# A two-layer streaming encoder: raw weights loaded ahead, the running streams' attention in four steps a pair, and a softmax that joins its two pieces by a reduction

## The chip, the cores and the metric

The kernel runs on one core of a Trainium2 chip. The metric is the device time of one execution in microseconds (us); the figure of merit is the median of three runs. Engines are named as in the profile: PE is TensorE (PEld its weight loads), DVE is VectorE, ACT is ScalarE, POOL is GpSimd, SP is SyncE, whose queue (SPq) issues all DMA transfers of this kernel in one order.

## The reference, cut to what matters

Two layers (`DEPTH = 2`) of width 1024. Each projects its tokens with `w_in`, feeds three groups of attention heads, gates each group, projects the mix with `w_out` and normalises. One call serves two requests with the same weights: 1024 new frames (`prompt`), and 8 running streams of 16 frames with 512 cached frames each (`sample`, 128 rows).

```
h = x @ w_in                                  # split into c_q, c_kv, k_rope, g_mla, f_q, f_k, ..., g_mem
mk, mv = mem @ w_mem_kv                       # 256 memory rows, 4 heads of 64
o_mla = attend(q, k_mla, v, chunk causal)     # 4 heads of 128 + 64 rotary
o_fox = attend(fq, fk, fv, causal, + cq[t] - ck[s])   # 4 heads of 64, with forget sums
o_mem = softmax(mq @ mk.T * scale) @ mv       # 4 heads of 64 over the memory
mixed = concat(o_mla * silu(g_mla), o_fox * silu(g_fox), o_mem * silu(g_mem))
y = layer_norm(alpha * x + mixed @ w_out) * ln_g + ln_b
```

For the sample the same weights are used, and the keys and values of the cache stand ahead of the new ones. The outputs are both `y` and the new cache rows of both layers.

## The kernel before, in words

**Precision and tiles.** Most projections are computed as three matmuls on a high and a low part (`mm3`, L188: L192 high by high, L193 and L194 the crossed ones). `wsplit` (L182) makes the two parts of a weight from its raw load: ACT casts (L183, tile `wh`), then DVE or POOL subtracts (L186, tile `wl`); `self.wdve` says which (1 is DVE, 0 is POOL, 2 takes turns). `WM0 = 2` sets it for the memory weights of layer 0. `split` (L172) does the same for activations (L176 on ACT, L177 on DVE).

**Slots.** Tiles come from pools with a fixed number of slots, and a load into a slot waits until the last reader of its former tile is done: `w` has 8 slots of 128x1024 (raw weights and their halves, tile inputs of the tail, and `lg`/`lb`, the norm's gain and bias), `pw` 5 (`x`, `memx`, softmax rows `pa`, tail inputs `xr`), `ptw` 2 (the transposed probabilities of the prompt's attention), `x` 12 of 128x512 (memory, and the sample's `kT` and `vraw`). The program is written as generators, one piece of background work at each `yield`; a scheduler then sets the order on each engine.

**Start of layer 0.** `main` calls `xload(0)` (L1442: two halves of the first 256 token columns, `x`), then `layer`, whose `gates` (L342) prepares `w_ge` by `wprep` (L259: load raw, split, for two halves of 4x256 rows each) and multiplies it with the tokens, 24 matmuls of 128x256 for each output tile, while `more` loads the other tokens. After `GE0 = 4` steps `mem_prep` (L281) loads `memx` and `w_mk`, projects the memory's keys, then loads `w_mv` and projects its values. Both weights' raw loads go into `w` slots at the place where they are split.

**Middle.** Memory attention, two halves of the forget attention (`fox`), the low-rank projections, then the MLA attention: 16 units (4 heads by 4 pairs of 128 queries, `mla_attn`, L875 on), each a softmax over 128 to 1024 keys in one or two pieces (`soft`, L394). For two pieces DVE takes the maximum of each (L402), joins the two by a 128x1 `tensor_tensor` (L404), ACT exponentiates (L406), DVE joins the two sums (L408), takes the reciprocal (L383), and POOL scales the row in place (L384), which is what PE transposes next (L201); PE then multiplies by the values into the one `pso` slot that DVE reads (L911). At head 3 `wout` (L1211) loads and splits the output weights, `wol` on POOL (L186).

**The sample.** Its attention is a generator, `sample`, that is advanced between other units: kinds `mem`, `fox` and `mla`, for each four pairs of streams. A pair takes one step for each key load, then one for the scores, one for the transposes and the value loads (`s_pv`, L977), one for the value matmuls, one for the output; its scores start when the former pair is finished. The counts `PER`, `PERF`, `PERL`, `PERQ`, `PERT` say how many steps are made at each MLA unit (4), fox unit (1), low-rank step (2), MLA projection (2) and tail tile (8).

**Tail.** Nine tiles of 128 rows: 48 matmuls of 128x512, residual and norm (L1257 to L1265, `lg` and `lb`), and the store of the row, in layer 0 to `yd`. `prep` loads a tile's mix `g` and residual `xr` one tile ahead. In layer 0 the rows of the first four tiles stay in `pw` until they are transposed for layer 1 (`xpair`), the others come back from `yd`. At tiles 4, 6 and 8 (`EM`) the next layer's `mem_prep` is advanced by a step: memory loads and splits, then keys, then values. Then layer 1 starts with `w_ge`.

Of the kernel before, what the change touches and what calls it, by code (L numbers as in the profile page):

```python
# [15 lines left out]
P = 128  # L16
# [4 lines left out]
TS = 16  # L21
# [24 lines left out]
PER = 4  # L46
PERF = 1
BGF = True
PERL = 2
PERQ = 2  # L50
# [19 lines left out]
WM0 = 2  # L70
# [10 lines left out]
class Enc:  # L81
# [40 lines left out]
    def ptw(self):  # L122
        return self.sp.tile([P, 2, 512], F32R, tag="ptw", bufs=T_SLOTS, name=self.nm("ptw"))
# [157 lines left out]
    def mem_prep(self, l):  # L281
        nc = self.nc
        M = []
        for a in range(2):
            raw = self.pw([P, 4, 256], name="memx")
            self.load(raw, self.i["mem_t"][a])
            for b in range(2):
                hi, lo = self.x([P, 2, 256], F32R, "mxh"), self.x([P, 2, 256], F32R, "mxl")
                self.split(hi, lo, raw[:, 2 * b:2 * b + 2, :])
                M.append((hi, lo))  # L290
        yield
# [8 lines left out]
        W = self.wprep(self.i["w_mk"][l])  # L300
# [14 lines left out]
        W = self.wprep(self.i["w_mv"][l])  # L315
# [26 lines left out]
    def gates(self, l, X, src, chunks, more=None):  # L342

        nc = self.nc
        W = self.wprep(self.i[src][l])
# [48 lines left out]
    def soft(self, pss, p, n, col=None, cut=None):  # L394
# [3 lines left out]
        nmx, sm = col(2), col(2)  # L398
        cut = cut or self.cuts(n)
        two = len(cut) == 2  # L400
        for x, (a, b) in enumerate(cut):
            nc.vector.tensor_reduce(nmx[:, x:x + 1], pss[x][:, :b - a], axis=AX, op=ALU.max, negate=True)  # L402
        if two:
            nc.vector.tensor_tensor(nmx[:, 0:1], nmx[:, 0:1], nmx[:, 1:2], op=ALU.min)  # L404
        for x, (a, b) in enumerate(cut):
            nc.scalar.activation(p[:, a:b], pss[x][:, :b - a], AF.Exp, bias=nmx[:, 0:1], accum_out=sm[:, x:x + 1])  # L406
        if two:
            nc.vector.tensor_tensor(sm[:, 0:1], sm[:, 0:1], sm[:, 1:2], op=ALU.add)  # L408
        self.norm(p[:, :n], sm[:, 0:1], col)
# [567 lines left out]
    def s_pv(self, p, nk, src, new, heads):  # L977
# [4 lines left out]
        ph = self.spr()  # L982
        for g in range(0, nkb, 4):
            pt = self.psx()
            k = min(4, nkb - g)
            for a in range(k):
                self.tr(pt[:, a * P:(a + 1) * P], p[:, (g + a) * P:(g + a + 1) * P])
            self.nc.vector.tensor_copy(ph[:, g * P:(g + k) * P], pt[:, :k * P])
        V = [[self.s_256(src(b, a), "vraw") for a in range(nk)] for b in range(2)]
        yield  # L990
        po = self.psx()[:, 0:P if heads else 256]
        for kb in range(nkb):
            first, last = kb == 0, kb == nkb - 1
            for b in range(2):
                v = V[b][kb // 2][:, kb % 2, :] if kb < 2 * nk else new
                if heads:
                    for c in range(2):
                        r = self.s_row(b, c)
                        self.mm(po[r, :], ph[:, kb * P + r.start:kb * P + r.stop], v[:, c * P:(c + 1) * P], first, last)
                else:  # L1000
                    r = slice(b * 64, b * 64 + 64)
                    self.mm(po[r, :], ph[:, kb * P + b * 64:kb * P + b * 64 + 64], v, first, last)
        yield
        s = self.xst([P, 256], name="so")
        w = P if heads else 256
# [26 lines left out]
    def s_mem(self, l):  # L1032
# [577 lines left out]
```

## Time and profile before

| what | value |
|---|---|
| median of 3 runs | 1501.42 us (1500.66 to 1505.01) |
| the profiled execution, its own time | 1506.76 us |
| its span in the profile | 1504.8 us |
| PE busy | 1421.8 us, 94% |
| DVE busy | 777.0 us, 52% |
| ACT busy | 617.8 us, 41% |
| POOL busy | 511.0 us, 34% |
| DMA, mean over the span | 120 GB/s |

The profiled execution is one run, 5.3 us above the median, and 2.0 us of it lie outside the span. A share of busy time is an average: PE leaves only 83.0 us of the span idle, so what is to be read is where these lie and what ended each. A row of a list gives start, duration, engine, line, operation, written tile and read tiles, and in brackets the idle time of the engine just before and what ended it. "PEclk" is the clock granted to PE as a share of full speed in a stretch.

### The profile page before, as it was taken

To read this page: it belongs to the slowest core of one execution; us is meant where nothing else is said; L and a number is where in the kernel's file an instruction comes from. 1 tells how busy PE (TensorE), PEld (TensorE's weight loads), DVE (VectorE), ACT (ScalarE), POOL (GpSimd) and SP (SyncE) were. 2 spreads that over 40 slices of the span, in tenths; PEclk is the share of its full clock that TensorE was granted. 3 is DMA by queue.
4 is the path that set the end of the run, shared out by engine and by line. 5 is a ranking of instruction groups with operands and counts; after the bars stand their busy time and mean duration, and the time that the engine had idled before them with its cause. 6 is when DMAs were issued, how large, how long until landed. Compare 5 with 4: busy or idle time off the path is not lost.

```text
span 1504.8 us, 27868 instructions
## 1 busy us (share of the span) xinstructions
PE 1421.8 (94%) x10222; PEld 1269.3 (84%) x10222; DVE 777.0 (52%) x1957; ACT 617.8 (41%) x1622; POOL 511.0 (34%) x740
## 2 busy tenths in 40 slices
PE   5899999999999999799799999999999999997997
PEld 4899889988987778688689989899889887786886
DVE  4235545255344655757444364552643556567565
ACT  5354445354254444532124453553542544455100
POOL 0233245255262321611141332544433542226012
PEclk9999999999999999999999999999999999999999
DMA  6312342335354431444343223324452643324531
GB/s 246 115 58 72 90 133 65 125 123 152 87 157 156 142 116 34 165 168 144 123 154 98 66 78 112 100 76 120 126 171 65 193 148 119 118 86 143 172 133 56
DMA packets 142343, 180.63 MB, mean 120 GB/s; under 512 B 32384, under 2 KB 99776, under 8 KB 142208
## 3 DMA queue, kind: packets, MB, share of 16 engines
q1 hardware_dynamic: 142208, 178.86, 37.3%
q8 instruction: 81, 1.33, 0.4%
q14 instruction: 54, 0.44, 0.1%
HBM read 138.69 MB, written 40.12 MB: 119 GB/s over the span
## 4 chain that ended last, share of the span: by engine, by line
PE 79%; DMA 8%; DVE 5%; ACT 3%; issue 2%; POOL 2%; SPq 0%; POOLq 0%; DVEq 0%; ACTq 0%
PE pss L192 14%; PE pss L193 13%; PE pss L194 13%; PE pss L197 9%; PE pso L197 7%; PE pst L201 6%; PE psx L197 6%; PE psx L192 3%; PE psx L193 3%; PE psx L194 3%; POOL wl L186 1%; DMA raw<-in_w_kv_dram 1%; ACT wh L183 1%; DMA raw<-in_w_out_dram 1%; PE psx L201 1%
## 5 line engine op out<-in xcount | busy, mean ns | idle before, releaser
L186 POOL TENSOR_TENSOR wl<-raw,wh 128x1024 fp32r<-128x1024 f32 (+3 forms) x42 | 106.5, 2536 | 273.7 <-PE pss L194 77.3
L177 DVE TENSOR_TENSOR ptw<-pst,ptw 128x512 fp32r<-128x512 f32 (+1 forms) x192 | 121.7, 640 | 62.2 <-ACT ptw L176 60.9
L176 ACT CAST ptw<-pst 128x512 fp32r<-128x512 f32 (+1 forms) x192 | 103.2, 550 | 87.4 <-PE pst L201 74.1
L192 PE MATMUL psx<-xh,wh 128*128 128x256 f32 x384 | 110.1, 287 | 16.9 <-ACT wh L183 14.5
L192 PE MATMUL pss<-wh,xh 128*128 128x306 f32 (+1 forms) x384 | 118.4, 308 | 0.0
L193 PE MATMUL pss<-wl,xh 128*128 128x306 f32 (+1 forms) x384 | 117.9, 307 | 0.0
L194 PE MATMUL pss<-wh,xl 128*128 128x306 f32 (+1 forms) x384 | 117.0, 305 | 0.0
L192 PE MATMUL pss<-woh,msh 128*128 128x512 f32 x288 | 115.5, 401 | 1.6 <-DVE xr L1257 1.6
L194 PE MATMUL pss<-woh,msl 128*128 128x512 f32 x288 | 114.7, 400 | 0.0
L193 PE MATMUL pss<-wol,msh 128*128 128x512 f32 x288 | 114.6, 398 | 0.0
L192 PE MATMUL pss<-xh,wh 128*128 128x256 f32 x384 | 111.8, 291 | 0.1
L193 PE MATMUL pss<-xl,wh 128*128 128x256 f32 x384 | 109.5, 285 | 0.0
L194 PE MATMUL pss<-xh,wl 128*128 128x256 f32 x384 | 109.2, 284 | 0.0
L193 PE MATMUL psx<-xl,wh 128*128 128x256 f32 x384 | 109.1, 284 | 0.0
L194 PE MATMUL psx<-xh,wl 128*128 128x256 f32 x384 | 108.5, 285 | 0.1
L384 POOL TENSOR_SCALAR pa<-pa,col 128x128 f32<-128x128 f32 (+3 forms) x64 | 47.8, 750 | 155.0 <-DVE col L383 123.6
L183 ACT CAST wh<-raw 128x1024 fp32r<-128x1024 f32 (+3 forms) x50 | 54.6, 1091 | 109.2 <-DMA raw<-in_w_mk_dram 31.6
L192 PEld LDWEIGHTS psx<-xh,wh 128*128 128x128 f32 x384 | 73.7, 192 | 18.0 <-ACT wh L183 14.7
L197 PE MATMUL pso<-ptw,vh 128*128 128x256 f32 (+1 forms) x336 | 75.0, 297 | 11.4 <-DVE g L911 4.3
L192 PEld LDWEIGHTS pss<-xh,wh 128*128 128x128 f32 x384 | 73.6, 192 | 3.3 <-issue 0.8
L406 ACT ACTIVATE pa<-pss,col 128x512 f32<-128x512 f32 (+3 forms) x96 | 55.3, 581 | 51.2 <-DVE col L404 27.3
L192 PEld LDWEIGHTS pss<-wh,xh 128*128 128x128 f32 x384 | 72.5, 189 | 1.8 <-issue 1.6
(365 smaller groups left out, 4256.1 us busy)
## 6 DMA issues: line engine op xcount, KB each, us to landing
gd<-gg SPq DMA_DIRECT2D x64, 128.0 KB
kT<-in_fox_kt_dram SPq DMA_DIRECT2D x32, 256.0 KB
vraw<-in_fox_v_dram SPq DMA_DIRECT2D x32, 256.0 KB
kT<-in_mla_kt_dram SPq DMA_DIRECT2D x32, 256.0 KB
vraw<-in_mla_v_dram SPq DMA_DIRECT2D x32, 256.0 KB
raw<-in_w_out_dram SPq DMA_DIRECT2D x16, 512.0 KB
g<-md SPq DMA_DIRECT2D x16, 512.0 KB
raw<-in_w_lr_dram SPq DMA_DIRECT2D x8, 612.0 KB
```

The lines of the kernel that those rows point to most:

```text
L176: nc.scalar.copy(hi, ps)
L177: nc.vector.tensor_tensor(lo, ps, self.f(hi), op=ALU.subtract)
L183: self.nc.scalar.copy(hi, raw)
L186: (self.nc.vector if dve else self.nc.gpsimd).tensor_tensor(lo, raw, self.f(hi), op=ALU.subtract)
L192: self.nc.tensor.matmul(ps, ah, bh, start=first and x == 0, stop=False)
L193: self.nc.tensor.matmul(ps, ah, bl, start=False, stop=False)
L194: self.nc.tensor.matmul(ps, al, bh, start=False, stop=last and x == n - 1)
L197: self.nc.tensor.matmul(ps, lhsT, rhs, start=start, stop=stop)
L201: self.nc.tensor.transpose(out, in_, self.ident[:k, :k])
L384: self.nc.gpsimd.tensor_scalar(p, p, rs, 1.0, op0=ALU.mult, op1=ALU.mult)
L406: nc.scalar.activation(p[:, a:b], pss[x][:, :b - a], AF.Exp, bias=nmx[:, 0:1], accum_out=sm[:, x:x + 1])
```

## The change

- **Start.** `xload(0)` issues the raw load of each half of `w_ge` right behind the same half of `x` (`wload`), and `wprep` takes these tiles and splits each in two pieces of 128x512.
- **Memory weights.** `mem_prep` loads the two raw halves of `w_mk` into the two `ptw` slots before its first `yield`, and those of `w_mv` into the same slots as soon as `w_mk` is split. `WM0` is 1: DVE makes the low parts in layer 0.
- **Tail.** `lg` and `lb` lie in `pw` slots, not in `w` slots, so that three of five `pw` slots are left for the tail's rows, `memx` and `x`.
- **Softmax.** The two maxima and the two sums are joined by a 128x2 `tensor_reduce` into a third column, where a `tensor_tensor` of two columns stood.
- **Sample.** `s_pairs` takes four steps a pair: scores, then transposes, then value matmuls, then output. The values of a pair and the keys of the next are loaded in the step of its scores. The counts are `PER` 1, `PERL` 1, `PERQ` 0.

The matmuls are the same in both programs.

The core of the diff (the forms of `s_mem`, `s_fox`, `s_mla` follow `s_pairs`):

```diff
-PER = 4
+PER = 1
 PERF = 1
-PERL = 2
-PERQ = 2
+PERL = 1
+PERQ = 0
-WM0 = 2
+WM0 = 1
-    def ptw(self):
-        return self.sp.tile([P, 2, 512], F32R, tag="ptw", bufs=T_SLOTS, name=self.nm("ptw"))
+    def ptw(self, shape=(P, 2, 512), dt=F32R, name="ptw"):
+        return self.sp.tile(list(shape), dt, tag="ptw", bufs=T_SLOTS, name=self.nm(name))
+    def wload(self, src, alloc=None):
+        parts, _, kn, n = src.shape
+        raws = []
+        for a in range(parts):
+            raw = (alloc or self.w)([P, kn, n if n <= P or n > 256 else 256], name="raw")
+            self.load(raw[:, :, :n], src[a])
+            raws.append(raw[:, :, :n])
+        return raws
-    def wprep(self, src):
+    def wprep(self, src, raws=None, pieces=1):
+        for raw in raws or self.wload(src):
...
-            self.wsplit(hi[:, :, :n], lo[:, :, :n], raw[:, :, :n])
+            for a in range(0, kn, kn // pieces):
+                k = slice(a, a + kn // pieces)
+                self.wsplit(hi[:, k, :n], lo[:, k, :n], raw[:, k])
# mem_prep
+        alloc = lambda shape, name: self.ptw(shape, F32, name)
+        raws = self.wload(self.i["w_mk"][l], alloc)
         yield
...
-        W = self.wprep(self.i["w_mk"][l])
+        W = self.wprep(None, raws)
+        raws = self.wload(self.i["w_mv"][l], alloc)
...
-        W = self.wprep(self.i["w_mv"][l])
+        W = self.wprep(None, raws)
# soft
-        nmx, sm = col(2), col(2)
+        nmx, sm = col(3), col(3)
+        one = slice(2, 3) if two else slice(0, 1)
...
-            nc.vector.tensor_tensor(nmx[:, 0:1], nmx[:, 0:1], nmx[:, 1:2], op=ALU.min)
+            nc.vector.tensor_reduce(nmx[:, one], nmx[:, 0:2], axis=AX, op=ALU.min)
...
-            nc.vector.tensor_tensor(sm[:, 0:1], sm[:, 0:1], sm[:, 1:2], op=ALU.add)
-        self.norm(p[:, :n], sm[:, 0:1], col)
+            nc.vector.tensor_reduce(sm[:, one], sm[:, 0:2], axis=AX, op=ALU.add)
+        self.norm(p[:, :n], sm[:, one], col)
# the sample: s_pairs in place of s_pv and of the steps in s_mem, s_fox, s_mla
+    def s_pairs(self, load, scores, nk, src, new, heads, out):
+        K = load(0)
+        yield
+        for p in range(4):
+            pr = scores(p, K)
+            V = [[self.s_256(src(2 * p + b, a), "vraw") for a in range(nk)] for b in range(2)]
+            if p < 3:
+                K = load(p + 1)
+            yield
...
# tail_start
-        lg = self.w([P, D], name="lg")
+        lg = self.pw([P, D], name="lg")
-        lb = self.w([P, D], name="lb")
+        lb = self.pw([P, D], name="lb")
# xload
+                if j == 0:
+                    raws.extend(self.wload(i["w_ge"][0][kh:kh + 1]))
```

Three places of the order show what moves. The first is SP's queue at the start of layer 0 before; `raw` with `in_w_ge` are the two halves of the gate weights, `x` the token halves, `memx` the memory.

```order
L164 DMA x_102<-in_x_t_dram 128x1024
L164 DMA x_110<-in_x_t_dram 128x1024
L164 DMA raw_139<-in_w_ge_dram 128x1024
L164 DMA x_151<-in_x_t_dram 128x1024
L164 DMA x_159<-in_x_t_dram 128x1024
L164 DMA x_227<-in_x_t_dram 128x1024
```

The next rows of the same queue after some constants, still before:

```order
L164 DMA x_235<-in_x_t_dram 128x1024
L164 DMA qg_5149<-in_mla_q_norm_dram 128x3x1
L164 DMA memx_306<-in_mem_t_dram 128x1024
L164 DMA raw_145<-in_w_ge_dram 128x1024
L164 DMA memx_316<-in_mem_t_dram 128x1024
```

And now, from the first load on:

```order
L164 DMA x_102<-in_x_t_dram 128x1024
L164 DMA raw_104<-in_w_ge_dram 128x1024
L164 DMA x_112<-in_x_t_dram 128x1024
L164 DMA raw_114<-in_w_ge_dram 128x1024
L164 DMA x_155<-in_x_t_dram 128x1024
L164 DMA x_163<-in_x_t_dram 128x1024
L164 DMA x_231<-in_x_t_dram 128x1024
```

The first half of `w_ge` moved from third to second place among the large loads, the second half from behind a `memx` to fourth place. The two `w_mk` loads stand behind the sixth `x` now, ahead of both `memx`.

The second place is SP's queue at the end of layer 0's tail, around tiles 4 to 6; `yd_97` is the store of tile 4's row. Before:

```order
L167 DMA yd_97<-xr_8669 128x1024
L164 DMA xr_9107<-in_x_sample_dram 128x1024
L164 DMA x_9327<-yd_97 128x1024
L164 DMA raw_8948<-in_w_mk_dram 128x1024
L167 DMA yd_98<-xr_8774 128x1024
L164 DMA x_9329<-yd_98 128x1024
L164 DMA raw_8954<-in_w_mk_dram 128x1024
```

And now (the `w_mk` loads, `raw_8800` and `raw_8802`, stand ahead of the store of tile 0):

```order
L164 DMA raw_8964<-in_w_mv_dram 128x1024
L164 DMA xr_8778<-in_x_prompt_dram 128x1024
L164 DMA memx_8780<-in_mem_t_dram 128x1024
L167 DMA yd_97<-xr_8673 128x1024
L164 DMA memx_8790<-in_mem_t_dram 128x1024
L164 DMA xr_8875<-in_x_prompt_dram 128x1024
L164 DMA g_9107<-gtd_142 128x1024
L164 DMA raw_8966<-in_w_mv_dram 128x1024
L164 DMA xr_8948<-in_x_prompt_dram 128x1024
L167 DMA yd_98<-xr_8778 128x1024
```

The `w_mk` loads are no longer behind the read of `yd_97`; the second half of the memory (`memx_8790`) is behind its store, since it takes the slot of the row that `yd_97` stores. On PE the key projection of the next layer begins behind tile 5 in both programs. Before (`pss_8899` is tile 5, `pss_9037` tile 6, `mxh_8778` the high part of the first quarter of the memory, `wh_8950` that of the first half of `w_mk`):

```order
L193 MATMUL pss_8899<-wol_8018,msh_8769 128x512
L194 MATMUL pss_8899<-woh_8017,msl_8770 128x512
L192 MATMUL pss_8960<-wh_8950,mxh_8778 128x256
L192 MATMUL pss_8997<-wh_8950,mxh_8778 128x256
L192 MATMUL pss_9037<-woh_7975,msh_8862 128x512
L193 MATMUL pss_9037<-wol_7976,msh_8862 128x512
```

And now, at the point where it turns to the second memory half (`mxh_8792` is the high part of the first piece of `memx_8790`; `pss_9045` is tile 6):

```order
L192 MATMUL pss_9045<-woh_7924,msh_8870 128x512
L193 MATMUL pss_9045<-wol_7925,msh_8870 128x512
L192 MATMUL pss_8968<-wh_8960,mxh_8792 128x256
L192 MATMUL pss_9005<-wh_8960,mxh_8792 128x256
L193 MATMUL pss_8968<-wl_8961,mxh_8792 128x256
L193 MATMUL pss_9005<-wl_8961,mxh_8792 128x256
L194 MATMUL pss_9045<-woh_7924,msl_8871 128x512
```

Before, two matmuls with the first half of `w_mk` stood right behind tile 5, and ahead of all of tile 6. Now 24 matmuls with the first memory half stand there, then 20 of tile 6, and behind these the first ones with the second memory half.

The third place is POOL in head 3 of the MLA attention of layer 0, where the `wol` subtractions stand between the norms of the probability rows `pa`. Before:

```order
L384 TENSOR_SCALAR pa_7822<-pa_7822,col_7827 128x384
L186 TENSOR_TENSOR wol_7976<-raw_7973,woh_7975 128x1024
L384 TENSOR_SCALAR pa_7837<-pa_7837,col_7842 128x512
L186 TENSOR_TENSOR wol_7982<-raw_7979,woh_7981 128x1024
L384 TENSOR_SCALAR pa_7904<-pa_7904,col_7913 128x896
L186 TENSOR_TENSOR wol_7988<-raw_7985,woh_7987 128x1024
L186 TENSOR_TENSOR wol_7994<-raw_7991,woh_7993 128x1024
L186 TENSOR_TENSOR wol_8000<-raw_7997,woh_7999 128x1024
L384 TENSOR_SCALAR pa_7929<-pa_7929,col_7938 128x1024
```

And now:

```order
L186 TENSOR_TENSOR wol_7889<-raw_7886,woh_7888 128x1024
L186 TENSOR_TENSOR wol_7895<-raw_7892,woh_7894 128x1024
L397 TENSOR_SCALAR pa_7712<-pa_7712,col_7717 128x384
L186 TENSOR_TENSOR wol_7901<-raw_7898,woh_7900 128x1024
L397 TENSOR_SCALAR pa_7727<-pa_7727,col_7732 128x512
L186 TENSOR_TENSOR wol_7907<-raw_7904,woh_7906 128x1024
L397 TENSOR_SCALAR pa_7804<-pa_7804,col_7813 128x896
L186 TENSOR_TENSOR wol_7913<-raw_7910,woh_7912 128x1024
L186 TENSOR_TENSOR wol_7919<-raw_7916,woh_7918 128x1024
L186 TENSOR_TENSOR wol_7925<-raw_7922,woh_7924 128x1024
L397 TENSOR_SCALAR pa_7829<-pa_7829,col_7838 128x1024
```

Two of them are ahead of the 384-key norm (L397 is the former L384), and still three in a row are ahead of the 1024-key norm.

More of the change, by code (lines that the diff above doesn't have):

```diff
@@ new lines, in s_pairs @@
+        w = P if heads else 256
+        K = load(0)
[6 more added lines that the diff above has]
+            yield
+            ph = self.spr()
+            for g in range(0, nkb, 4):
+                pt = self.psx()
+                k = min(4, nkb - g)
+                for a in range(k):
+                    self.tr(pt[:, a * P:(a + 1) * P], pr[:, (g + a) * P:(g + a + 1) * P])
+                self.nc.vector.tensor_copy(ph[:, g * P:(g + k) * P], pt[:, :k * P])
+            yield
+            po = self.psx()[:, 0:w]
+            for kb in range(nkb):
+                first, last = kb == 0, kb == nkb - 1
+                for b in range(2):
+                    v = V[b][kb // 2][:, kb % 2, :] if kb < 2 * nk else new
+                    if heads:
+                        for c in range(2):
+                            r = self.s_row(b, c)
+                            self.mm(po[r, :], ph[:, kb * P + r.start:kb * P + r.stop], v[:, c * P:(c + 1) * P], first, last)
+                    else:
+                        r = slice(b * 64, b * 64 + 64)
+                        self.mm(po[r, :], ph[:, kb * P + b * 64:kb * P + b * 64 + 64], v, first, last)
+            s = self.xst([P, 256], name="so")
+            self.nc.scalar.copy(s[:, 0:w], po)
+            yield
+            pt = self.psx()
+            for c in range(w // P):
+                self.tr(pt[:, c * P:(c + 1) * P], s[:, c * P:(c + 1) * P])
+            out(p, pt)
+            yield
@@ new lines, in load @@
+        def load(p):
+            K = [[self.s_256(kv("fox_kt", 2 * p + b, a), "kT") for a in range(2)] for b in range(2)]
+            ck = self.x([P, 512], name="sck")
+            cn = self.xst([P, TS], name="scn")
+            src = self.cumd[8 * p:8 * p + 8, :]
+            row = lambda a, b: bass.AP(tensor=src.tensor, offset=src.offset + a, ap=[[528, 8], [0, TS], [1, b - a]])
+            self.load(ck, row(0, 512))
+            self.load(cn, row(512, 528))
+            return K, self.s_q(1, 2, p), ck, cn, self.mask(1, p)
@@ L1132, in s_mla @@
+        return self.s_pairs(load, scores, 2, lambda b, a: kv("fox_v", b, a), new[:, 1, :], True,
+                            lambda p, pt: self.s_diag(pt, self.otf, p))
     def s_mla(self, l):
@@ L1179, in sample @@
     def sample(self, l):
[L1181 to L1206 removed]
+        yield from self.s_mem(l)
+        while self.stage < 1:
+            yield
+        self.nc.gpsimd.tensor_copy(self.otf[:, 2:4], self.sx[:, 0, :].rearrange("p (c t) -> p c t", c=2))
+        yield from self.s_fox(l)
+        while self.stage < 2:
+            yield
+        yield from self.s_mla(l)
         self.s_mla_out(l)
@@ L1278, in tail, with layer @@
             outtile(i, *ready[i])
-    def layer(self, l, X, xin, after, early, more=None):
+    def layer(self, l, X, xin, after, early, more=None, raws=None):
         nc = self.nc
@@ L1312, in layer @@
         self.wdve = WG1 if l else 1
-        ge = self.gates(l, X, "w_ge", (6, 7), more)
+        ge = self.gates(l, X, "w_ge", (6, 7), more, raws)
         if l == 0:
```

177 lines of the change are left out of this document (47 added, 130 removed).

## The prediction

> **What bounds the kernel now.** I read the page's busy shares first, then what PE waited for over the whole span, then the stretches in which those waits lie, and in these the rows in order of time.
>
> ```profile
> PE 1421.8 (94%) x10222; PEld 1269.3 (84%) x10222; DVE 777.0 (52%) x1957; ACT 617.8 (41%) x1622; POOL 511.0 (34%) x740
> ```
>
> PE is the bound, and the change leaves its matmuls as they are. So all that can be won is in 1504.8 - 1421.8 = 83.0 us of idle PE, and in the time that a lowered clock stretches its work. The list of what PE waited for (total, times, longest):
>
> ```profile
> PE psx L192 <- ACT wh L183: 17.4, 4, 9.3
> PE pss L192 <- ACT wh L183: 7.8, 2, 6.9
> PE pss L197 <- ACT pa L406: 5.1, 4, 2.3
> PE pso L197 <- DVE g L911: 4.3, 2, 2.2
> PE psx L193 <- POOL wl L186: 4.0, 2, 2.3
> PE pss L192 <- ACT qn L831: 4.0, 2, 3.0
> PE psx L197 <- DMA vraw<-in_mem_v_dram: 1.9, 2, 1.0
> ```
>
> Weights that are not ready (`wh`, `wl`) make 29 us of the 83, and DVE's and ACT's part in the MLA softmax 9. Five stretches hold these waits; a row gives the stretch, its length, PE busy, then the other engines, the granted clock, the DMA share and GB/s:
>
> ```profile
> 0.00:60.00 60.00, 37.83 (x251) 35.22 (x252) 23.55 (x37) 26.96 (x44) 7.50 (x12) 0.89 0.56 193
> 600.00:650.00 50.00, 40.75 (x254) 35.90 (x253) 36.55 (x80) 29.54 (x66) 28.95 (x21) 0.97 0.46 161
> 720.00:740.00 20.00, 12.99 (x50) 9.90 (x48) 7.92 (x13) 1.85 (x3) 1.70 (x2) 0.83 0.52 184
> 740.00:760.00 20.00, 18.55 (x91) 15.31 (x92) 7.49 (x11) 1.05 (x1) 6.28 (x4) 1.00 0.31 105
> 760.00:780.00 20.00, 18.29 (x99) 15.63 (x98) 10.47 (x14) 5.31 (x9) 9.01 (x6) 0.91 0.46 139
> 1350.00:1400.00 50.00, 40.97 (x257) 35.95 (x256) 35.29 (x71) 28.48 (x61) 27.48 (x19) 0.97 0.48 162
> ```
>
> PE idles 22.2 us in the first stretch (60 - 37.83), 10.2 in 720 to 780 (the turn from layer 0 to layer 1), 9.3 and 9.0 in the two stretches of MLA head 3: 50.7 of 83. The change works on all of them.
>
> **The start.** In order of time:
>
> ```profile
> 4.80 2.40 ACT L176 CAST xh<-x 128x512 fp32r<-128x512 f32 x4 [2.80 <-DMA x<-in_x_t_dram]
> 8.23 1.04 ACT L183 CAST wh<-raw 128x1024 fp32r<-128x1024 f32 x1 [1.03 <-DMA raw<-in_w_ge_dram]
> 9.33 0.58 PE L192 MATMUL psx<-xh,wh 128*128 128x256 f32 x1 [9.33 <-ACT wh L183]
> 18.24 1.05 ACT L183 CAST wh<-raw 128x1024 fp32r<-128x1024 f32 x1 [0.16 <-DMA raw<-in_w_ge_dram]
> 19.34 0.58 PE L192 MATMUL psx<-xh,wh 128*128 128x256 f32 x1 [5.22 <-ACT wh L183]
> 37.74 0.39 PE L193 MATMUL psx<-wl,mxh 128*128 128x256 f32 x1 [2.29 <-POOL wl L186]
> ```
>
> The first large load is in at 4.8, the third (half of `w_ge`) at 8.2, so each takes 1.7. As the second load it is in at 6.5; its first piece is cast in half of 1.04, so PE starts at about 7.1 and 2.2 us are gone. The second half is the fourth load, in at 9.9 where it was 18.2, and split by about 12, when PE still has matmuls of the first half (it ran from 9.33 to 14.1 on them, 4.8 us): the gap of 5.22 goes but for some 0.5. The waits for the memory weights, 22.2 - 9.3 - 5.2 = 7.7 with small ones, go where the raw loads are early and DVE takes POOL's place. What is late next: all data come through a queue that is full in this stretch,
>
> ```profile
> 9.33:20.00 10.67, 5.41 (x27) 4.92 (x28) 8.09 (x12) 7.22 (x12) 0.00 (x0) 0.81 0.99 372
> 46.50:53.50 7.00, 5.18 (x23) 4.89 (x24) 0.29 (x1) 1.44 (x3) 3.31 (x3) 0.52 0.21 82
> ```
>
> (DMA share 0.99), and `w_mk` now stands ahead of both `memx`. With six `x`, two `w_ge`, two `w_mk` and two `memx`, the twelfth large load is in at about 4.8 + 11 x 1.7 = 23.5, and `w_mv` behind that. I leave 3.5 us for such new waits. Idle then is 7.1 + 0.5 + 3.5 = 11 against 22.2: 11 gained. The clock: 0.89 over 60 us is 6.6 us of withheld pulses, of which PE's busy share (0.63) is 4.2; I take 3. Sum 14; bounds 8 (new waits of 6.5 and the clock as now, 11 - 3) and 19 (no new wait, whole clock).
>
> The dip at 46.5 to 53.5 came at a clock of 0.52 although PE was busy 5.18 of 7. The Trainium skill, "TensorE: Matmul & The Clock Gate", section "What's actually happening", lets the clock fall only after an idle window of about 3.4 us; PE's longest gap there was under 2, so the trace does not bear the rule out. By the rule no dip would stay at the start and the 4.2 would be gained whole, sum 15; I go by the row, that short gaps close together can do it, and keep a part.
>
> **The turn to layer 1.**
>
> ```profile
> 720.80 0.42 SPq L167 DMA_DIRECT2D yd<-xr  x1
> 725.87 0.33 SPq L164 DMA_DIRECT2D x<-yd  x1
> 726.29 0.38 SPq L164 DMA_DIRECT2D raw<-in_w_mk_dram  x1
> 730.71 1.04 ACT L183 CAST wh<-raw 128x1024 fp32r<-128x1024 f32 x1 [9.60 <-DMA raw<-in_w_mk_dram]
> 730.86 0.33 SPq L167 DMA_DIRECT2D yd<-xr  x1
> 731.81 0.79 PE L192 MATMUL pss<-wh,mxh 128*128 128x256 f32 x2 [6.91 <-ACT wh L183]
> ```
>
> SP's queue waits for the store of tile 4 to land (720.80 to 725.87, 5.07 us) before it may read it back, and `w_mk` is behind that; it lands at 730.7, and PE, two of whose matmuls stand ahead of tile 6, idles from 724.9 to 731.8. Now `w_mk` is loaded before tile 0's store. What is late next is the second memory half: it takes the slot of tile 4's row, so it is issued at about 726, lands at 730.4 (4.4 as above) and is split by about 732 (0.6 on ACT, 0.7 on DVE). Ahead of it PE has 24 matmuls of 128x256 and 20 of 128x512.
>
> ```profile
> L192 PE MATMUL pss<-woh,msh 128*128 128x512 f32 x23 | 9.3, 404 | 1.6 <-DVE xr L1257 1.6
> L192 PE MATMUL pss<-wh,mxh 128*128 128x256 f32 x8 | 2.3, 282 | 0.0
> ```
>
> These are from 740 to 760, with two more rows each for L193 and L194: 67 wide and 24 narrow in 18.55 us, so 18.55 / (67 + 12) = 0.235 a wide one, 0.117 a narrow one. The cover is 24 x 0.117 + 20 x 0.235 = 7.5 us, from 724.9 to 732.4, which just hides it; were tile 6 not there, 7 us would be idle as now. The other rows of tail 0 are read back from `yd` in three slots, and PE's order has their transposes between the first `w_ge` matmuls: up to 4 us may show there. Gain: 10.2 idle plus clock (0.83 in 20 us at a busy share of 0.65, and 0.91 at 0.91: 2.2 + 1.6) is 14.0; I take 9, bounds 4 and 14.
>
> **MLA head 3.** The costs of the join, over both layers, and one chain of time:
>
> ```profile
> L383 DVE RECIPROCAL col<-col 128x1 f32<-128x1 f32 x128 | 20.5, 161 | 37.8 <-ACT pf L420 25.8 <-ACT pa L406 5.9 <-ACT sx L1030 1.4
> L404 DVE TENSOR_TENSOR col<-col 128x1 f32<-128x1 f32 x32 | 16.9, 527 | 0.7
> L408 DVE TENSOR_TENSOR col<-col 128x1 f32<-128x1 f32 x32 | 11.8, 370 | 10.9 <-ACT pa L406 10.7
> 615.99 7.03 POOL L186 TENSOR_TENSOR wol<-raw,woh 128x1024 fp32r<-128x1024 f32 x3
> 616.15 2.20 DVE L404 TENSOR_TENSOR col<-col 128x1 f32<-128x1 f32 x1
> 618.27 0.41 DVE L911 TENSOR_TENSOR g<-pso,g 128x256 f32<-128x256 f32 x1
> 618.83 0.48 PE L197 MATMUL pso<-ptw,vh 128*128 128x256 f32 x2 [2.16 <-DVE g L911]
> 620.80 0.27 DVE L383 RECIPROCAL col<-col 128x1 f32<-128x1 f32 x2
> 624.93 1.87 DVE L404 TENSOR_TENSOR col<-col 128x1 f32<-128x1 f32 x1
> 627.57 0.39 PE L197 MATMUL pss<-xnh,xnh 128*128 128x256 f32 x1 [2.23 <-ACT pa L406]
> ```
>
> An operation on 128x1 needs 0.16, yet L404 needs 2.20 while POOL subtracts `wol`; the reciprocal, with one input in SBUF, runs unhindered in the same POOL burst (620.80). So 16.9 + 11.8 - 64 x 0.16 = 18.5 us of DVE time is being held. The new reduction is not in this trace: between 0.16 (the reciprocal) and 2.20 (L404, held). I take 0.16, since the reciprocal too reads one tile from SBUF. The Trainium skill, "SBUF — State Buffer", section "Who interferes with whom", says that a DVE operation with two SBUF inputs contends with a POOL operation that reads SBUF, and that a `tensor_reduce` on trn2 never does; the trace agrees for the two forms it has, and by the rule the term stays as it is. On the path: the wait of 2.16 falls to some 0.2 (L911 2.0 earlier), that of 2.23 by 1.7 (ACT's `pa` stood behind the join of 1.87), and about 1.3 of the smaller ones: 5 a layer. What stays is POOL's norm behind three `wol` in a row, 7.03 us. Sum 10; bounds 3 (the next waits move up) and 17 (all of 18.3).
>
> **The rest.** Value loads a step earlier remove 1.9 (`vraw`). Sample matmuls leave the low-rank and query steps, where PE waits 4.0 for `qn`, and spread over the MLA units: up to 4 either way, taken at -1. Sum +1.
>
> **The sum.** 14 + 9 + 10 + 1 = 34. The profiled execution took 1506.8, so 1472.8 like for like; it lies 5.3 above the median, so 1467.5.
>
> **The rivals.**
> - *The full queue hides the early weights* (chance 0.15). For it: a DMA share of 0.99 until 20 us. Against: the gap of 5.22 came of the order of the loads, not of their rate, and 22.2 - 9.3 - 5.2 = 7.7 of the idle lies behind that gap. Start 5 in place of 14: 1476.5.
> - *POOL's norm becomes the bound in head 3* (0.15): the 7.03 us of `wol` delay the next probability row whatever DVE does. Against it: PE takes that row a unit later. 0 to 3 in place of 10: about 1476.
> - *Both* (0.07): 1485.
> - *More goes than I allow* (0.05): upper bounds at all three places, 1451.5.
> - *The edits do not reach PE* (0.03): the waits come back elsewhere, within 4 us of 1501.4.
> - *The tail's three slots decide* (0.05), the case on the other side. A slot's round is load 4.4, the tile's matmuls 48 x 0.235 = 11.3, norm 6 (tile 5's matmuls end at 724.9, its store is issued at 730.86), landing 5.07: 26.8, under 3 x 11.3 = 33.9 for three slots. A row that is held 11.3 more for its partner's transposes (tiles 0 to 3 of layer 0) makes 38.1. From 33.9 on PE loses the excess once in three tiles, six times in the two tails; at 41.4, 3.3 more for loads that queue behind a store's landing, that is 6 x 7.5 = 45 lost against 34 won: 1512. Against it: only four of 18 tiles are held.
>
> **The numbers.** The forecast has 0.50, so 1467.5 is the predicted time. The range takes in the two single rivals, their pair and the bounds of the terms that can fall together: 1453 to 1490. Under 0.3% (4.5 us) a measurement of this kernel can't be told from no change: faster 0.92, same 0.03, slower 0.05.
>
> **What would show it.** Right: the first matmul at 7 to 7.5 and no gap over 2 us until 25; no wait for `wh` of 6.9 at the turn; the join at 0.16 to 0.2 while POOL subtracts `wol`, and PE idle of 3 to 5 in each head 3. Wrong: PE waits for `mxh` or `xr` of over 3 us in the tails, a join still over 0.5, or PE idle above 62 us in all.

## The result: 37 us faster, and the profile after

| what | before | after |
|---|---|---|
| median of 4 runs | 1503.22 us (1500.66 to 1505.25) | 1465.78 us (1463.54 to 1469.0) |
| the profiled execution | 1506.76 us | 1465.12 us |
| its span | 1504.8 us | 1463.3 us |
| PE idle in the span | 83.0 us | 54.4 us |

The kernel before has a fourth run here, 1505.25, beside the three shown above. The ratio is 0.9753, 95% interval 0.9727 to 0.978. The predicted time was 1467.5.

First the busy shares on the page of the changed kernel:

```profile
PE 1408.9 (96%) x10222; PEld 1262.3 (86%) x10222; DVE 765.9 (52%) x1961; ACT 617.5 (42%) x1624; POOL 505.6 (35%) x738
```

PE's matmuls are the same 10222, and they take 12.9 us less (1421.8 - 1408.9); idle time fell by 28.6. The two make 41.5, the difference of the spans. The same matmuls take less because the clock is lowered less often (0.984 of full speed over the span before, 0.992 after).

To see where that lies, both programs are cut at places that PE reaches with the same work done: the first matmul of the memory attention, the first score matmul of the MLA attention, its last value matmul, and the same in layer 1. What remains is the tail of layer 1. Of the kernel before (start and end, length, then busy time and count for PE, PEld, DVE, ACT and POOL, then the granted clock, the DMA share and GB/s):

```profile
0.00:74.20 74.20, 52.03 (x371) 49.42 (x372) 25.65 (x42) 30.27 (x51) 11.21 (x14) 0.91 0.54 182
74.20:508.00 433.80, 420.15 (x3345) 388.81 (x3344) 207.43 (x602) 199.11 (x566) 176.42 (x292) 0.99 0.37 111
508.00:665.10 157.10, 147.85 (x978) 122.76 (x977) 96.76 (x249) 74.30 (x190) 48.38 (x47) 0.99 0.38 126
665.10:821.20 156.10, 145.93 (x829) 126.22 (x829) 84.87 (x129) 34.73 (x57) 32.99 (x30) 0.97 0.40 132
821.20:1249.90 428.70, 418.17 (x3347) 386.89 (x3345) 206.88 (x602) 198.91 (x565) 176.28 (x292) 1.00 0.37 113
1249.90:1406.80 156.90, 147.87 (x978) 122.81 (x976) 96.81 (x249) 74.07 (x190) 48.42 (x47) 0.99 0.38 126
```

And the same stretches of the changed kernel:

```profile
0.00:60.60 60.60, 49.95 (x371) 48.66 (x371) 28.15 (x46) 29.87 (x53) 6.81 (x12) 0.94 0.63 223
60.60:490.50 429.90, 415.92 (x3347) 386.23 (x3345) 208.59 (x602) 199.82 (x566) 175.59 (x292) 1.00 0.38 113
490.50:643.20 152.70, 148.72 (x977) 123.30 (x976) 89.00 (x250) 73.44 (x190) 48.30 (x47) 0.99 0.38 125
643.20:785.50 142.30, 141.81 (x830) 123.60 (x830) 85.62 (x128) 34.78 (x57) 33.43 (x30) 1.00 0.45 149
785.50:1213.80 428.30, 415.29 (x3347) 386.33 (x3345) 208.20 (x602) 199.79 (x565) 175.94 (x292) 1.00 0.37 113
1213.80:1365.10 151.30, 147.14 (x977) 121.78 (x976) 88.81 (x251) 73.44 (x190) 48.41 (x47) 1.00 0.40 127
```

PE's counts agree row for row within two, so the lengths may be compared. I call the rows start, middle 0, MLA 0, turn, middle 1 and MLA 1. The start is 13.6 us shorter, the turn 13.8, the two MLA rows 4.4 and 5.6, the middles 3.9 and 0.4. The tail of layer 1 is what is left of each span, 98.0 (1504.8 - 1406.8) and 98.2 (1463.3 - 1365.1). In the turn PE now idles 0.5 us of 142.3, where it idled 10.2, and the clock is whole.

What PE waits for longest in the changed kernel (total, times, longest):

```profile
PE psx L192 <- ACT wh L183: 7.2, 2, 6.6
PE pss L197 <- DVE qf L352: 6.0, 2, 3.3
...
PE pss L197 <- ACT pa L420: 1.7, 4, 0.5
```

The waits for `wh` of 17.4 and 7.8, for `wl` of 4.0, for the join's `pa` of 5.1 and for `qn` of 4.0 are gone or small. What stands at the head is the first load (6.6 of the 7.2), and a wait for `qf`, which I had not looked at; experiment 12 comes back to it.

The start of the changed kernel: ACT's cast of the second half of `w_ge`, and the two matmuls ahead of which PE waited longest.

```profile
9.78 1.14 ACT L183 CAST wh<-raw 128x512 fp32r<-128x512 f32 x2
```

```profile
6.60 0.58 PE L192 MATMUL psx<-xh,wh 128*128 128x256 f32 x1 [6.60 <-ACT wh L183]
...
15.99 0.39 PE L192 MATMUL psx<-xh,wh 128*128 128x256 f32 x1 [1.77 <-DVE gg L376]
```

PE starts at 6.60 where it started at 9.33. The second half of `w_ge` is cast by 10.9, when PE still has matmuls of the first, so the gap of 5.22 is gone. The longest gap left, 1.77, is ended by DVE's gate and not by a weight.

The turn, from the rows of SP's queue and of PE around tile 5:

```profile
696.13 0.37 SPq L164 DMA_DIRECT2D memx<-in_mem_t_dram  x1
697.76 0.33 SPq L167 DMA_DIRECT2D yd<-xr  x1
702.86 0.38 PE L192 MATMUL pss<-wh,mxh 128*128 128x256 f32 x1
703.37 0.33 SPq L164 DMA_DIRECT2D memx<-in_mem_t_dram  x1
```

The second memory half still waits for the store's landing (697.76 to 703.37, 5.61 us), as the prediction had it. But PE begins the keys at 702.86 without a wait for weights, and has the first memory half and tile 6 to work on until the second half is split; no gap over 0.5 is left in the turn.

### The profile page after: what moved, and what is told of

Same layout as the page of the kernel before. It is cut to its first block, busy times and chain, and to the rows that moved or that the text cites. A ratio compares the mean times of both kernels' runs of the same rounds, so it can differ in the third digit from the quotient of the medians.

```text
span 1463.3 us, 27842 instructions
## 1 busy us (share of the span) xinstructions
PE 1408.9 (96%) x10222; PEld 1262.3 (86%) x10222; DVE 765.9 (52%) x1961; ACT 617.5 (42%) x1624; POOL 505.6 (35%) x738
## 4 chain that ended last, share of the span: by engine, by line
PE 80%; DMA 6%; DVE 5%; ACT 3%; POOL 2%; issue 2%; SPq 1%; POOLq 0%; DVEq 0%; ACTq 0%
PE pss L192 13%; PE pss L194 13%; PE pss L193 13%; PE pss L197 9%; PE pso L197 7%; PE pst L201 6%; PE psx L197 6%; PE psx L192 4%; PE psx L194 4%; PE psx L193 4%; SPq L164 1%; PE psx L201 1%; DMA scq<-cumd 1%; DMA raw<-in_w_out_dram 1%; DMA x<-in_x_t_dram 1%
## 5 line engine op out<-in xcount | busy, mean ns | idle before, releaser
L186 POOL TENSOR_TENSOR wl<-raw,wh 128x1024 fp32r<-128x1024 f32 (+3 forms) x40 | 101.5, 2541 | 232.5 <-ACT wh L183 124.1
L397 POOL TENSOR_SCALAR pa<-pa,col 128x128 f32<-128x128 f32 (+3 forms) x64 | 47.9, 757 | 139.5 <-DVE col L396 94.4
L193 PEld LDWEIGHTS pss<-xl,wh 128*128 128x128 f32 x384 | 73.8, 192 | 0.3
```

The source lines that it names most:

```text
L186: (self.nc.vector if dve else self.nc.gpsimd).tensor_tensor(lo, raw, self.f(hi), op=ALU.subtract)
L193: self.nc.tensor.matmul(ps, ah, bl, start=False, stop=False)
L397: self.nc.gpsimd.tensor_scalar(p, p, rs, 1.0, op0=ALU.mult, op1=ALU.mult)
```

## The experiments

All times are medians. "Ratio" is the ratio to the kernel before on the same chip, with its 95% interval. Experiments 1 to 4 ran on one chip, 5 to 8 on another, 9 to 11 on a third, 12 on a fourth. A difference of two ratios from different groups is uncertain by about 0.0035, or 5 us.

### 1. The reduction alone, in the kernel before

The edit is made in the kernel before, in both places of `soft`, and nothing else:

```diff
-            nc.vector.tensor_tensor(nmx[:, 0:1], nmx[:, 0:1], nmx[:, 1:2], op=ALU.min)
+            nc.vector.tensor_reduce(nmx[:, one], nmx[:, 0:2], axis=AX, op=ALU.min)
```

> The kernel before, with the join of the two softmax pieces made by the reduction of a 128x2 tile into a third column, and nothing else. My theory: what held DVE was the second input from SBUF while POOL subtracts; the join takes 0.15 us also in the POOL bursts of head 3, PE's idle time there falls from 8.9 and 8.7 us to 3 to 4 in each layer, and the time falls by 8 to 12 us (ratio to before 0.992 to 0.995). Rival: the idle time of head 3 went because the sample's matmuls now reach into head 3 and fill it; then the join is short here too, but PE's idle time in head 3 stays over 7 us in each layer and the time within 4 us of before.

Measured: 1491.27, ratio 0.9922 (0.9891 to 0.9952), 11.7 us less. DVE's groups of the two joins in this kernel (count, then busy time in all and mean ns of one):

```profile
L409 DVE TENSOR_REDUCE col<-col 128x1 f32<-128x2 f32 x32 | 4.9, 152 | 11.0 <-ACT pa L407 10.8
L405 DVE TENSOR_REDUCE col<-col 128x1 f32<-128x2 f32 x32 | 4.8, 150 | 0.7
```

They took 527 and 370 ns as `tensor_tensor`. And its MLA 0:

```profile
511.20:662.20 151.00, 147.50 (x978) 121.38 (x976) 87.46 (x250) 73.82 (x190) 48.35 (x47) 1.00 0.40 131
```

It is 6.1 us shorter than before, and MLA 1 is 6.0 (150.9). The new form of the two joins carries the whole gain in the MLA attention, with the old sample steps and the old order of loads, and PE idles 3.5 us in this stretch, so it is not the new sample steps that fill it. The prediction's rival, that POOL's three `wol` in a row hold the row anyway, falls too.

### 2. The changed kernel with the old join

The reverse edit, in the changed kernel.

> The changed kernel with the join made by a tensor_tensor of two columns again. My theory: the joins under POOL's wol subtractions take 1 to 2.2 us again, PE idles 7 to 9 us in each head 3 where it idles 3.0 now, and the time rises by 8 to 12 us, to 1474 to 1478. Rival (filler from the sample): the joins are long again, but the time stays within 4 us of the changed kernel's 1465.8.

Measured: 1474.03, ratio 0.9796 (0.9766 to 0.9827), 8.3 us over the changed kernel's first measurement. On the same chip, the changed kernel with the join of experiment 3 had 0.9728; the difference is 10 us. In head 3 of layer 0, POOL's subtraction and the slowest join:

```profile
600.16 4.75 POOL L186 TENSOR_TENSOR wol<-raw,woh 128x1024 fp32r<-128x1024 f32 x2
601.80 3.13 DVE L422 TENSOR_TENSOR col<-col 128x1 f32<-128x1 f32 x1 [0.31 <-ACT pa L420]
```

The same place in the changed kernel:

```profile
596.45 0.14 DVE L418 TENSOR_REDUCE col<-col 128x1 f32<-128x2 f32 x1
596.46 7.06 POOL L186 TENSOR_TENSOR wol<-raw,woh 128x1024 fp32r<-128x1024 f32 x3
599.95 0.15 DVE L422 TENSOR_REDUCE col<-col 128x1 f32<-128x2 f32 x1 [0.59 <-ACT pa L420]
```

One number is joined in 3.13 us or in 0.15, beside POOL operations of the same kind (the 3.13 reach over two of them, of 2.4 each). The time came out as expected, the idle time did not:

```profile
490.70:647.60 156.90, 152.12 (x977) 123.39 (x976) 94.86 (x250) 73.86 (x190) 48.39 (x47) 0.99 0.37 121
```

The stretch is as long as before the change, but PE idles only 4.8 of it, and its same matmuls take 152.12 where the changed kernel has 148.72. The clock does not explain it, since it is 0.99 over this row in both kernels; what lengthens them stays open.

### 3. Another join that is not held: a tensor_scalar

```diff
-            nc.vector.tensor_reduce(nmx[:, one], nmx[:, 0:2], axis=AX, op=ALU.min)
+            nc.vector.tensor_scalar(nmx[:, one], nmx[:, 0:1], nmx[:, 1:2], None, op0=ALU.min)
```

> The changed kernel with the join made by a tensor_scalar: one column as input, the other as the number per partition. If DVE is held only by a second tensor stream from SBUF (my theory), the join takes 0.15 to 0.25 us in POOL's bursts and the time is that of the changed kernel, 1462 to 1470. If any second operand fetched from SBUF holds it, the joins take up to 2.2 us and the time is 1474 to 1478. No run so far shows an operation of this form beside POOL.

Measured: 1463.46, ratio 0.9728 (0.97 to 0.9756), as the changed kernel. One line's operations, with the shortest, the median and the longest in ns:

```profile
L418 DVE TENSOR_SCALAR col<-col x32: 201/214/216, 494.8 to 1339.3; 128x1 f32<-128x1 f32 x32
```

The longest of 32 is 216 ns, and so it is for the 32 joins of the sums (L422). Of these 64, 12 start inside a `wol` subtraction of POOL; in the kernel before 14 did, and none of those took less than 754 ns. So none was held here, though two columns of SBUF are read: one as tensor, one as the scalar operand. It is not the reduction that frees the path, but that the second number is not a second tensor.

### 4. The old sample steps in the changed kernel

`s_pv` and the old steps back, and the old counts:

```diff
-PER = 1
+PER = 4
-PERL = 1
-PERQ = 0
+PERL = 2
+PERQ = 2
```

> The changed kernel with the sample's attention as before: a step for each key load, values loaded behind the transposes, and the counts 4, 2 and 2 at MLA units, low-rank steps and MLA projections. My theory: the steps are worth little, the time is 1464 to 1471; the waits for vraw (1.9 us in all) and qn (4.0) come back, those for POOL's h (4.9) shrink, and head 3 still idles 3 to 5 us a layer. Rival: the new steps fill head 3; then its idle time rises to 7 or more a layer and the time to 1474 or more.

Measured: 1470.78, ratio 0.9783 (0.9749 to 0.9818): 4.5 us by ratio over the first measurement of the changed kernel, though the intervals overlap. Its middle 0 and middle 1:

```profile
60.30:492.10 431.80, 417.96 (x3346) 386.66 (x3345) 205.15 (x602) 199.49 (x566) 175.63 (x292) 0.99 0.37 112
788.70:1221.30 432.60, 418.97 (x3347) 388.39 (x3345) 205.79 (x602) 199.26 (x565) 175.58 (x292) 0.99 0.37 112
```

The middles are 1.9 and 4.3 longer than after the change, the MLA stretches are as there (152.9 and 150.9 against 152.7 and 151.3). That the new steps fill idle time in the MLA attention is refuted. What they bring in the middles is not the waits that I had named: the one for `vraw` did not come back, and that for `qn` is 0.4 us. PE idles 27.4 us in the two middles, where the changed kernel idles 27.0; 5.7 of the 6.2 us are busy time, with the clock lowered for 17 us in all against 7. Where the steps act is not shown, and it is one profile of each.

### 5 to 8. The turn and the start, one part each

Experiment 6 puts the norm's gain and bias back into `w` slots:

```diff
-        lg = self.pw([P, D], name="lg")
+        lg = self.w([P, D], name="lg")
```

Experiment 7 loads the memory weights where they are split, and makes `wprep` load one half at a time, as before the change:

```diff
-        raws = self.wload(self.i["w_mk"][l], alloc)
-        W = self.wprep(None, raws)
+        W = self.wprep(self.i["w_mk"][l])
# wprep
-        for raw in raws or self.wload(src):
+        parts = len(raws) if raws else src.shape[0]
+        for x in range(parts):
+            raw = raws[x] if raws else self.wload(src[x:x + 1])[0]
```

Experiment 5 is 6 and 7 together, with the `wprep` lines. Experiment 8 has the `wprep` lines of 7, keeps the early memory weights, and loads `w_ge` in `gates` again:

```diff
-                if j == 0:
-                    raws.extend(self.wload(i["w_ge"][0][kh:kh + 1]))
```

> The changed kernel with the raw memory weights loaded into w slots at the place where they are split, each half at its own split, and with the norm's gain and bias in w slots, as before. My theory: the wait of 6.9 us for wh at the turn comes back with the smaller ones (10 us idle and a clock dip of 3 to 4), and 2 to 4 us of the waits for the memory weights at the start: 1478 to 1484 against 1465.8. Rival: the turn was shortened by something else (the order of the rows' read-back): 1466 to 1472.

> The changed kernel with only the norm's gain and bias back in w slots (five pw slots free in the tail), the raw memory weights still in ptw. My theory says that the early load of the memory weights is what counts at the turn, and w slots and pw slots little: PE idles under 3 us at the turn, 1462 to 1471. Rival: the w slots that the move frees are what lets the weights be split early; then the turn idles 6 us or more, 1473 to 1480.

> The changed kernel with only the raw memory weights back in w slots and loaded at their split, each half at its own; gain and bias stay in pw. SP's order has the first half of w_mk ahead of tile 4's store here, since w slots are free, and the second half behind it. My theory (the load that is ahead of the store hides the wait, wherever its slot is): the turn idles 1 to 5 us, the start 2 to 4 more than in the changed kernel, 1468 to 1475. Rival (the ptw slots are needed): the wait of 6 to 7 us at the turn is back, 1478 or more.

> The changed kernel with w_ge loaded in gates as before, each half at its own split and in one piece; the memory weights stay early and on DVE. My theory: first matmul at 9.3, the gap of about 5 us behind it is back, the clock dips once more, the start is 7 to 11 us longer, 1473 to 1477. Rival (a full queue hides it all): what is early at the start only waits elsewhere in the first 60 us, 1464 to 1469.

| experiment | median | ratio | what |
|---|---|---|---|
| 5 | 1475.78 | 0.9807 (0.9792 to 0.9822) | late memory weights, `wprep` lines, gain and bias in `w` |
| 6 | 1465.64 | 0.974 (0.9713 to 0.9767) | gain and bias in `w` alone |
| 7 | 1464.55 | 0.9726 (0.9706 to 0.9746) | late memory weights, `wprep` lines |
| 8 | 1466.57 | 0.9752 (0.9735 to 0.9768) | late `w_ge`, `wprep` lines |

The turn of 5:

```profile
642.80:796.70 153.90, 144.06 (x829) 124.76 (x829) 84.74 (x129) 34.70 (x57) 32.98 (x30) 0.98 0.41 134
```

In 5 the wait is back: 9.8 us of idle PE, one gap for `wh` of 6.7 among it. In 6 and 7 the turn takes 142.9 and 142.6, as in the changed kernel (142.3). SP's queue in 5 tells why:

```profile
698.67 0.42 SPq L167 DMA_DIRECT2D yd<-xr  x1
703.66 0.33 SPq L164 DMA_DIRECT2D x<-yd  x1
704.08 0.38 SPq L164 DMA_DIRECT2D raw<-in_w_mk_dram  x1
```

And in 7:

```profile
689.50 0.33 SPq L164 DMA_DIRECT2D raw<-in_w_mk_dram  x1
...
695.50 0.33 SPq L167 DMA_DIRECT2D yd<-xr  x1
```

In 5 `w_mk` stands behind the store and its reading back, as before. In 7 its load is still written at the split, but it goes into a `w` slot that gain and bias no longer hold, and is issued 14.6 us earlier (13.3, counted from where the turn begins in each), ahead of the store; the second half, at 702.29, stays behind the store and costs PE nothing that shows. So either edit alone mends the turn: a slot that comes free early, in `ptw` or in `w`, puts the load ahead of the store. Only where both are undone do 12.2 us come back (0.9807 - 0.9726). I had put the whole gain on the loads' place and none on the slots.

Experiment 8 did not cost the 7 to 11 us that I expected, although its start is 7.8 longer:

```profile
0.00:68.40 68.40, 50.20 (x371) 48.82 (x372) 27.94 (x44) 29.99 (x51) 7.00 (x12) 0.93 0.57 198
```

The gap behind the first half is back, 7.09 us long. Something in the kernel had become faster by as much. Experiments 5 and 7 were 2.2 and 3.5 us faster than their expected ranges too, although in 7 the start was 4.9 us longer (65.5). The three share the lines in `wprep`, which I had put in only to restore the order of the loads. That called for experiment 12. Against it, which has the same lines, experiment 8 is 0.9752 - 0.9691 = 0.0061 slower, or 9 us, and 7 is 5 us slower, from different chips.

### 9 to 11. The changed kernel again, the whole start undone, the negation

Experiment 9 is the changed kernel. Experiment 10 is 7 and 8 together with `WM0 = 2`: SP's first 33 rows are those of the kernel before. Experiment 11 tries a cause of the wait for `qf`, an added DVE operation that changes the sign of `scq` behind its load:

```diff
-        nc.vector.tensor_scalar(cq, cq, -1.0, None, op0=ALU.mult)
-            nc.gpsimd.tensor_scalar(pr[:, 0:512], ck, 1.0, cq[:, p:p + 1], op0=ALU.mult, op1=ALU.add)
+            nc.gpsimd.tensor_scalar(pr[:, 0:512], ck, 1.0, cq[:, p:p + 1], op0=ALU.mult, op1=ALU.subtract)
```

> The changed kernel as it is, beside the two that follow. All theories expect the ratio measured first, 0.973 to 0.978.

> The changed kernel with the whole start as before: w_ge and the memory weights loaded at their split, each half at its own, and POOL in turn for the memory weights; SP's order of the first 33 rows is that of before. Gain and bias stay in pw, so the turn stays short, as in the run with the memory weights in w. My theory: the start is 13 to 15 us longer, as before, and the time 10 to 14 us more than the changed kernel's. Rival: what is won at the start is partly given back in layer 0, as the runs with half of the start undone showed (7.8 us lost at the start, 3.1 less in the stretch behind it): 4 to 8 us more.

> The changed kernel without DVE's negation of the sample's forget sums (128x4), which waits for a DMA of these sums and has the low part of qf behind it on DVE, while PE waits 3.3 and 2.7 us for that; POOL subtracts the sums instead of adding the negated ones. My theory: PE's wait for qf falls from 6.0 us in all to under 2, and the time by 3 to 5 us, to a ratio of 0.970 to 0.973. Rival: PE waits as long for the next thing behind the same DMA (POOL's part of the scores): no difference.

Measured: 1466.33 and 0.9738 (0.972 to 0.9756) for 9; 1471.93 and 0.9782 (0.9758 to 0.9807) for 10; 1464.72 and 0.9731 (0.9707 to 0.9754) for 11. The start of 10 takes 76.4 at a clock of 0.89, where before it was 74.2 at 0.91. Against experiment 9 it costs only 6.6 us by ratio, in the rival's range and not in mine, because the `wprep` lines give some back; against experiment 12, which has the same lines, 0.9782 - 0.9691 = 0.0091, or 13.7 us, uncertain by 5. In 11 the waits for `qf` are gone, but two others stand in their place:

```profile
PE pss L192 <- DVE col L432: 5.9, 4, 2.4
PE pss L197 <- DVE col L432: 3.4, 4, 2.0
```

That is a later operation of DVE in the same chain. The time is unchanged, so the negation was not the cause.

### 12. Each half loaded when it is split

The three lines in `wprep` of experiment 7, alone, in the changed kernel. Early loads stay early; all other weights are loaded and split half by half, as before the change.

> The changed kernel with every weight that is not loaded ahead (all but w_ge of layer 0 and the memory weights) loaded and split one half after the other, as before; in the changed kernel wprep issues both raw halves first and then splits, so two raw tiles stand in w slots at once. In the five runs with halves loaded at their split the stretch from the memory attention to the MLA attention took 424 to 428 us a layer, in the six with both loads first 428 to 431. Theory: this is what was given back of the start's gain; the two stretches take 424 to 428.5, PE's wait for qf falls from 6.0 us to under 4.5, and the kernel is 3 to 6 us faster than the changed one, ratio 0.969 to 0.972. Rival: the stretch is shorter only where the start is longer, since the same transfers then have more time; then nothing changes, ratio 0.973 to 0.976.

Measured: 1455.68 (1453.78 to 1460.37), ratio 0.9691 (0.9666 to 0.9715). This beats both kernels: 7 us under experiment 9 by ratio (0.9738 - 0.9691), 9 under the first measurement (0.9753 - 0.9691). Its start and its two middles:

```profile
0.00:57.90 57.90, 47.84 (x371) 46.55 (x372) 28.34 (x46) 29.96 (x53) 7.10 (x12) 1.00 0.66 234
57.90:485.60 427.70, 414.45 (x3345) 385.68 (x3344) 205.98 (x602) 199.34 (x566) 175.41 (x292) 1.00 0.38 113
...
779.40:1204.00 424.60, 413.52 (x3346) 384.19 (x3345) 205.87 (x602) 198.83 (x565) 175.70 (x292) 1.00 0.38 114
```

The middles are 2.2 and 3.7 shorter, though the start is short here too (57.9): the rival falls. That holds over all runs: with these lines (5, 7, 8, 10, 12) the two middles together take 851.6 to 854.8, and without them, at the new sample steps (after, 2, 3, 6, 9, 11), 857.1 to 860.4. The start differs mostly by the clock (0.94 and 1.00): in experiment 9, without the lines, it takes 57.6.

One of the places where it comes from is the wait for `qf`. SP's queue in the changed kernel, then DVE and PE; `raw` is half of `w_kv`, `scq` four small loads:

```profile
178.13 0.36 SPq L164 DMA_DIRECT2D raw<-in_w_kv_dram  x1
...
180.26 3.63 SPq L164 DMA_DIRECT2D scq<-cumd  x4
188.67 0.54 DVE L1113 TENSOR_SCALAR scq<-scq 128x4 f32<-128x4 f32 x1 [4.99 <-DMA scq<-cumd]
...
189.82 0.30 PE L197 MATMUL pss<-fkh,qf 128*128 128x128 f32 x1 [3.29 <-DVE qf L352]
```

And in experiment 12:

```profile
177.34 0.38 SPq L164 DMA_DIRECT2D raw<-in_w_kv_dram  x1
177.82 2.60 SPq L164 DMA_DIRECT2D scq<-cumd  x4
183.11 0.34 SPq L164 DMA_DIRECT2D raw<-in_w_kv_dram  x1
184.12 0.33 DVE L1115 TENSOR_SCALAR scq<-scq 128x4 f32<-128x4 f32 x1 [4.76 <-DMA scq<-cumd]
186.56 0.30 PE L197 MATMUL pss<-fkh,qf 128*128 128x128 f32 x1 [2.39 <-DVE qf L354]
```

One half of `w_kv` is issued just ahead of `scq` in both. In the changed kernel that is the second half; now it is the first, and the second stands behind `scq` (183.11). The kernel before had it so too (halves at 193.63 and 200.00, `scq` at 194.11). From the first `scq` issue to DVE it takes 6.3 us where it took 8.4 (before the change 6.1), and PE waits 0.9 less. That the place of the second half is the reason is argued from these rows, not tested alone. It is only a part of the 7: over both layers the waits for `qf` fall from 6.0 to 3.8. In the two middles together PE idles 2.7 less and is busy 3.2 less; which of the other weights make up the rest was not taken apart.

## Why the prediction was right

**The start (14).** Right. Idle PE fell from 22.2 to 10.7, by 11.5 (predicted 11), and the clock gave 2.1 of busy time (predicted 3): 13.6 in the profiles. Experiments 10 and 12 give 13.7, from different chips and so uncertain by 5. The first matmul came at 6.60 (predicted 7.1). The new waits are 10.7 - 6.6 = 4.1 where I allowed 0.5 + 3.5. The rival of the full queue falls: from 6.60 to 20 us the DMA share is 0.99 in the changed kernel too, and the gain came all the same, so the gap of 5.22 was one of the order of the loads. What `WM0` brings by itself has no run.

**The turn (9, bounds 4 and 14).** The mechanism was right, the term was sized too small: 13.8. Of 14.0 I took off 5, since up to 4 us might show for transposes of rows that are read back from `yd`, and some of the clock; neither came. The cover for the second memory half, worked out as 7.5 us, held. What the prediction did not see is that the two edits do the same: by experiments 6 and 7 the memory weights need not lie in `ptw` when `lg` and `lb` leave `w`, and the reverse.

**The MLA join (10).** Right: 4.4 and 5.6 in the profiles, 11.7 by the reduction alone in experiment 1, 10 between experiments 2 and 3. PE idles 4.0 and 4.2 in the two stretches, as said (3 to 5). The join is at 0.15 beside POOL's subtraction, and the next wait that could have moved up, POOL's norm, did not.

**The rest (+1).** It came to 4.1 (3.9 + 0.4 - 0.2), and here the working failed, not the number; that it came near is luck, as two things that I did not have in the sum nearly offset each other. The two middles together took 862.5 before; without the cost of `wprep` they take 852.3 (experiment 12), and with it 858.2. So 10.2 were won, where I had taken +1. The sample's new steps are 6.2 of them by experiment 4 (864.4 against 858.2; 4.0 to 7.3 against the other runs with the new steps), though not by the waits that I named. The other 4.0 have no run of their own; the reduction alone shortens the middles by 1.1 (861.4 in experiment 1). And 5.9 were lost again in a place that I had not seen. The diff shows it: `for raw in raws or self.wload(src)` issues both loads ahead of the first split. I had read the helper as moving only the weights that are loaded early, though every weight goes through it.

**The sum.** 34 predicted, 37.4 measured in medians, 41.5 between the two profiled executions. With the loss in `wprep` mended, experiment 12 is 46 us under the kernel before on its chip (0.0309 of 1504.21), so part of the closeness comes of a loss that the sum did not have. The 1451.5 of the rival with all upper bounds leaves out the +1 of the rest. The rival on the other side, the tail's three slots, falls: with gain and bias back in `w`, so that the tail has all five `pw` slots, experiment 6 measures the same time.

## What to carry to other kernels

A 128x1 operation that takes ten times its usual time is likely being held: look for what runs beside it, and here, beside POOL's subtraction, give it a form with one tensor in SBUF before anything larger is rebuilt. When a load is moved ahead, look for every other caller of the helper that was changed for it: early is good for the few loads that are waited for, and a cost for those that then stand ahead of them in the queue. A gain from an earlier load can often be had by freeing a slot as well as by moving the issue, so undo each alone and both together.

## What the runs showed of the hardware

The clock. The prediction left open what lowers it. In all traces here a lowered stretch has a clock of 0.5 and lasts 3.4 us or two or three times that (the one at the end of each span aside), so the spans were cut into stretches of 3.4 us at these borders. Every lowered stretch that follows one at the full clock follows one in which PE was busy for at most 0.58 of the time; none follows a stretch with 0.61 or more. Up to 0.48, every one was followed by a lowered clock; between these, some were and some were not (1.68 of 3.40, or 0.49, in experiment 9 from 186.70 on was not). Before, at the start (1.57 of 3.41 is 0.46):

```profile
43.33:46.74 3.41, 1.57 (x13) 1.36 (x13) 0.36 (x1) 1.04 (x1) 0.14 (x1) 1.00 0.72 211
46.74:53.56 6.82, 5.08 (x23) 4.78 (x24) 0.29 (x1) 1.42 (x2) 3.23 (x3) 0.50 0.19 74
```

In experiment 12, in head 3 of the MLA attention (0.66):

```profile
590.00:593.41 3.41, 2.25 (x19) 2.05 (x17) 1.43 (x6) 1.64 (x4) 3.41 (x3) 1.00 0.86 288
593.41:596.82 3.41, 3.12 (x23) 2.88 (x24) 2.28 (x9) 3.41 (x10) 3.41 (x2) 1.00 0.21 64
```

In the changed kernel a stretch of 0.56 in the same head (1.91 of 3.41, from 597.42 on) was followed by 0.51. No empty stretch is needed: gaps of a microsecond or two that come close together came before a clock of one half for 3.4 us or more, and 3.4 us of full work at half the clock are 1.7 us more, on top of the gaps. So idle time that is taken away can give back more than its own length (in the turn 9.7 of idle and 4.1 of busy time). The executions of one kernel differ along with it: of the four of the changed kernel the shortest, 1463.54, had a mean clock of 0.995, and the longest, 1469.0, had 0.991. It is what these traces show, and was not tested by itself.

The Trainium skill, "TensorE: Matmul & The Clock Gate", section "What's actually happening", asks for an idle window of about 3.4 us; these rows speak against that, with PE busy at about half of the window.
